# Issuing TensorE's instructions in program order in the loop over expert units

## The chip, the cores and the metric

The kernel runs on one core of one Trainium2 chip. The metric is the device time of one execution in microseconds (us). TensorE (PE in the profile, PEld for its weight loads) does the matrix products, VectorE (DVE) and ScalarE (ACT) the elementwise work, GpSimd (POOL) almost nothing here, and SyncE (SP) issues nearly all transfers from memory.

## The reference, cut to what matters

Two layers of a transformer-like block over 256 latent and 256 context tokens of width 1024, all in float32. Each layer has a mixer (a gated recurrence, a windowed attention and a gated chunk mixer) and a channel mixer. The change is in the channel mixer of the second layer, which picks two of eight experts for each of the 256 latent tokens:

```python
def _swiglu(h, w_gate, w_up, w_down):
    return (jax.nn.silu(h @ w_gate) * (h @ w_up)) @ w_down

def _moe(h, router, w_gate, w_up, w_down):
    logits = (t @ router).astype(jnp.float32)
    top_val, top_idx = lax.top_k(logits, TOP_K)
    top_w = jax.nn.softmax(top_val, axis=-1)
    gate = jnp.sum(one_hot(top_idx, 8) * top_w[..., None], axis=1)
    for e in range(N_EXPERTS):
        out = out + gate[:, e:e + 1] * _swiglu(t, w_gate[e], w_up[e], w_down[e])
```

An expert is 1024 -> 3584 -> 1024, so its three matrices are 44 MB, and each token needs only two experts.

## The kernel before

Only the tokens that chose an expert are gathered for it, up to 96 of them (`S`), in three blocks of 32. Whether an expert has more than 64 tokens is read at run time (`self.third[e]`), and every product of the loop stands twice in the program, in the two arms of an `If` (`arms`): one arm works on three blocks, the other leaves the third out.

The hidden width of an expert is cut into four **units** u = 0 to 3: three of 1024 hidden columns and one of 512 (`UNITS`). A unit goes through these steps:

- `gate_up` (G below): the gate and up products into three PSUM banks of kind `u`, in two halves, each an `If` of its own. A half reads 8 weight tiles of 512 KB (4 in the last unit). Then ACT and DVE make `mh`, silu(gate) times up.
- `turned` (T): eight transposes (L1620, L1625; four in the last unit) of `mh` into the two PSUM banks of kind `t`, copied out as `mT`.
- `moe_down` (D): the down product of `mT` with 8 weight tiles (4 in the last unit), in one `If`, into two banks of kind `mm` in which all units of the expert add up.

After an expert's last D, `moe_out` reads the two `mm` banks into `y` (ACT and DVE) and `moe_add` splits `y` into `yhl` and adds it to the tokens: eight products (L1682, m below) through the two `t` banks, each pair followed by a DVE addition into `xt` (L1684). `moe_gather` (g, o: L1827, L1564) picks the tokens of the next two experts, through the same two banks.

In the Python program, D of a unit is written one unit late: G of unit u, D of unit u-1, T of unit u. The pieces of `moe_add` and `moe_gather` are generators in the queue `behind`; `paced` runs one piece of them after each half of G and after each D.

That is the order in which the program is traced. The order in which an engine issues its instructions is chosen afterwards by the framework's scheduler; an `If` block is moved as a whole. So TensorE's order before need not be the program's.

The weights come through a ring of 4 KB-per-partition slots (`Ring`, L179): SP issues each load into a slot that earlier products have read, in the order of use that `moe_plan` writes down. 672 loads of 512 KB feed the loop.

Of the kernel before, what the change touches and what calls it, by code (L numbers as in the profile page):

```python
# [21 lines left out]
P = 128  # L22
# [5 lines left out]
NE = 8  # L28
# [168 lines left out]
class Gen:  # L197
# [1766 lines left out]
    def moe_layer(self):  # L1964
        nc, tc, mem = self.nc, self.tc, self.mem
        xg = {}
        self.third = [nc.values_load(self.cnt[0:1, 9 + e:10 + e], min_val=0, max_val=1)
                      for e in range(NE)]
        self.run(self.moe_gather(0, 2, xg, self.sel, self.rank, S, self.map0))
        behind = deque()  # L1970

        def paced(g):
            for _ in g:
                if behind and next(behind[0], self) is self:
                    behind.popleft()
        pend = y = None

        def lower():
            nonlocal y
            e, u, hT = pend  # L1980
            if u == 0:
                y = self.psum("mm"), self.psum("mm")
            paced(self.moe_down(e, hT, u, *y))
            if u == 3:
                behind.append(self.moe_add(self.moe_out(*y), xg[e][1], self.gate[:, :, e:e + 1], S, xg[e][2]))
        for e, u in self.UNITS:
            if u == 0 and e % 2 and e + 1 < NE:
                behind.append(self.moe_gather(e + 1, 2, xg, self.sel, self.rank))
            h = mem.get(4, [P, 2, 512], "mh")
            paced(self.gate_up(e, xg[e][0], u, h))  # L1990
            if u == 3:
                mem.put(xg[e][0])
            if pend:
                lower()
            pend = e, u, self.turned(h, u)
        lower()
        self.run(*behind)
        self.ring.close()
        self.store()
        with tc.If(nc.values_load(self.cnt[0:1, 8:9], min_val=0, max_val=256) > S):  # L2000
            self.moe_rest()
            self.store()
# [114 lines left out]
```

## Time and profile before

| what | before |
|---|---|
| median of 3 runs | 1904.02 us (1901.4 to 1908.13) |
| the profiled execution: its time, its span | 1906.77 us, 1905.0 us |
| busy share of the span: PE, PEld, DVE, ACT | 93%, 57%, 41%, 28% |
| mean granted clock of TensorE | 0.974 of full |
| the loop over expert units | about 937.5 to 1886 us of the span |

The span runs from the first to the last instruction. "Busy" of PE is the time in which some product runs. [...] A wait is idle time of an engine and what released it; "issue" is idle time for which the profile shows no releaser.

### The profile page before, as it was taken

Reading aid. Unit: us, or ns where it says so; the run is one execution under the profiler, and the core shown is the slowest. Engines: PE = TensorE matmul, PEld = TensorE weight load, DVE = VectorE, ACT = ScalarE, POOL = GpSimd, SP = SyncE. Lnnn points to the kernel's source line nnn. Section 1 sums busy time; section 2 is a strip of 40 time slices with the busy share of each in tenths; the row PEclk is TensorE's granted clock in tenths of the full one; section 3 lists DMA queues with packets and bytes.
Section 4 is the critical chain, followed back from the end, with each engine's and each line's share of the span. In section 5 each row is a group of like instructions: output and inputs, shape, how many; then the busy total and the mean of one; then the engine's idle time right before and its main releaser. Section 6 shows DMA issues by size and latency. Waiting matters only on the chain. (4 is left out here: it accounts for less than half of the span.)

```text
span 1905.0 us, 34709 instructions
## 1 busy us (share of the span) xinstructions
PE 1773.4 (93%) x14056; PEld 1088.7 (57%) x14057; DVE 778.7 (41%) x1924; ACT 538.5 (28%) x1203; POOL 33.9 (2%) x56
## 2 busy tenths in 40 slices
PE   6999999999999999999899978999789997899896
PEld 3998779988788899998534322233222332233232
DVE  3656887998563578778400112001120021100201
ACT  4654646622223367575200101001010010100000
POOL 1000000100000000000000000000000000000000
PEclk9999999999999999999999999999899998999898
DMA  9224242377562254312789999999998999999780
GB/s 337 78 85 166 82 155 89 116 256 263 163 249 97 90 173 137 133 47 105 289 314 407 407 407 408 345 359 408 407 385 321 355 408 407 370 345 373 302 332 25
DMA packets 137007, 485.65 MB, mean 255 GB/s; under 512 B 15888, under 2 KB 17040, under 8 KB 136784
## 3 DMA queue, kind: packets, MB, share of 16 engines
q1 hardware_dynamic: 136080, 480.08, 67.0%
q8 instruction: 168, 2.75, 0.6%
q0 software_dynamic: 704, 2.36, 0.4%
q14 instruction: 55, 0.45, 0.1%
HBM read 481.33 MB, written 1.05 MB: 253 GB/s over the span
## 5 line engine op out<-in xcount | busy, mean ns | idle before, releaser
L1575 PE MATMUL u<-wr,xg 128*32 128x512 f32 (+1 forms) x5376 | 535.5, 553 | 32.3 <-issue 28.2
L1575 PEld LDWEIGHTS u<-wr,xg 128*32 128x32 f32 x5376 | 179.9, 113 | 375.5 <-issue 335.6
L1608 DVE TENSOR_TENSOR mh<-mh,u 128x512 f32<-128x512 f32 (+1 forms) x32 | 19.9, 621 | 643.5 <-PE u L1575 643.5
L1575 PE MATMUL mm<-wr,mT 128*32 128x512 f32 x2352 | 263.2, 599 | 0.7 <-ACT mT L264 0.3
L264 ACT ACTIVATE mh<-u 128x512 f32<-128x512 f32 (+1 forms) x64 | 34.6, 540 | 751.7 <-PE u L1575 751.2
L125 ACT ACTIVATE hi<-raw 128x512 fp32r<-128x512 f32 (+2 forms) x296 | 160.2, 580 | 249.5 <-PE u L246 87.4
L126 DVE TENSOR_TENSOR lo<-raw,hi 128x512 fp32r<-128x512 f32 (+2 forms) x296 | 178.5, 634 | 100.5 <-ACT hi L125 99.1
L1575 PEld LDWEIGHTS mm<-wr,mT 128*32 128x32 f32 x2352 | 76.3, 111 | 169.4 <-issue 160.3
L244 PE MATMUL u<-hx,hi 128*128 128x512 f32 (+1 forms) x384 | 142.8, 372 | 0.0
L245 PE MATMUL u<-hx,lo 128*128 128x512 f32 (+1 forms) x384 | 142.6, 371 | 0.0
L246 PE MATMUL u<-hx,hi 128*128 128x512 f32 (+1 forms) x384 | 142.6, 371 | 0.0
L245 PE MATMUL mm<-fx,lo 128*128 128x256 f32 (+1 forms) x264 | 85.6, 325 | 5.7 <-DVE lo L126 5.5
L244 PE MATMUL mm<-hi,hx 128*128 128x256 f32 x288 | 85.4, 298 | 4.1 <-ACT hx L264 3.8
L244 PE MATMUL mm<-fx,hi 128*128 128x256 f32 (+1 forms) x264 | 85.0, 322 | 0.6 <-ACT hi L125 0.6
L246 PE MATMUL mm<-fx,hi 128*128 128x256 f32 (+1 forms) x264 | 84.6, 321 | 0.0
L245 PE MATMUL mm<-hi,hx 128*128 128x256 f32 x288 | 82.2, 287 | 0.4 <-DVE hx L521 0.3
L246 PE MATMUL mm<-lo,hx 128*128 128x256 f32 x288 | 81.6, 285 | 0.0
L245 PEld LDWEIGHTS u<-hx,lo 128*128 128x128 f32 x384 | 72.3, 188 | 12.6
L246 PEld LDWEIGHTS u<-hx,hi 128*128 128x128 f32 x384 | 72.3, 188 | 12.4
L244 PEld LDWEIGHTS u<-hx,hi 128*128 128x128 f32 x384 | 72.3, 188 | 12.4
L447 DVE SCALAR_TENSOR_TENSOR adat<-adat,silb 128x1024 f32<-128x1024 f32 x56 | 68.3, 1222 | 15.9 <-DMA adat<-in_w_adaT 15.1
L244 PE MATMUL u<-hi,hx 128*128 128x256 f32 x256 | 74.1, 290 | 0.1
(342 smaller groups left out, 2514.7 us busy)
## 6 DMA issues: line engine op xcount, KB each, us to landing
wr<-in_moe_g SPq DMA_DIRECT2D x224, 512.0 KB, 9.9
wr<-in_moe_u SPq DMA_DIRECT2D x224, 512.0 KB, 9.0
wr<-in_moe_d SPq DMA_DIRECT2D x224, 512.0 KB, 9.5
adat<-in_w_adaT SPq DMA_DIRECT2D x56, 512.0 KB, 4.9
raw<-in_ffn_gu SPq DMA_DIRECT2D x44, 512.0 KB, 3.5
adaw<-in_w_ada SPq DMA_DIRECT2D x40, 512.0 KB, 5.8
raw<-in_w_in SPq DMA_DIRECT2D x40, 512.0 KB, 3.8
raw<-in_ffn_d SPq DMA_DIRECT2D x24, 384.0 KB, 3.5
```

What stands on the lines that cost most here:

```text
L125: nc.scalar.activation(h[:, s], r[:, s], AF.Copy)
L126: nc.vector.tensor_tensor(l[:, s], r[:, s], h[:, s].bitcast(F32), op=ALU.subtract)
L244: i = mm(ps, lh, rh, start=start, stop=False, skip_group_check=True)
L245: mm(ps, ll, rh, start=False, stop=False, skip_group_check=True)
L246: self.final = mm(ps, lh, rl, start=False, stop=stop, skip_group_check=True)
L264: i = self.nc.scalar.activation(out, in_, func, **kw)
L447: nc.vector.scalar_tensor_tensor(w[i] if z == zs - 1 else junk, w[i], 1.0, sil[z], op0=ALU.mult, op1=ALU.mult, accum_out=self.mods[l][:, c ...
L1575: self.nc.tensor.matmul(bank[c:c + 32, :n], lhsT, rhs, start=start, stop=stop, tile_position=(0, c), skip_group_check=True)
L1608: nc.vector.tensor_tensor(h[:, 0, :n], h[:, 0, :n], U[:, :n], op=ALU.mult)
```

## The change

The loop over units is wrapped in a block that tells the framework to keep TensorE's instructions in the order in which they are traced. The statements in it are the same; the other engines are still ordered by the scheduler.

```diff
-        for e, u in self.UNITS:
-            if u == 0 and e % 2 and e + 1 < NE:
-                behind.append(self.moe_gather(e + 1, 2, xg, self.sel, self.rank))
-            h = mem.get(4, [P, 2, 512], "mh")
-            paced(self.gate_up(e, xg[e][0], u, h))
-            if u == 3:
-                mem.put(xg[e][0])
-            if pend:
-                lower()
-            pend = e, u, self.turned(h, u)
-        lower()
+        with tc.manual_schedule(engines={mybir.EngineType.PE}):
+            for e, u in self.UNITS:
+                if u == 0 and e % 2 and e + 1 < NE:
+                    behind.append(self.moe_gather(e + 1, 2, xg, self.sel, self.rank))
+                h = mem.get(4, [P, 2, 512], "mh")
+                paced(self.gate_up(e, xg[e][0], u, h))
+                if u == 3:
+                    mem.put(xg[e][0])
+                if pend:
+                    lower()
+                pend = e, u, self.turned(h, u)
+            lower()
```

TensorE's rows at the start of the third expert (e = 2), before: the end of the previous expert's last D, T of the new expert's unit 0, three products of `moe_add` for the expert just ended (`yhl` times `ohT`), and the first half of unit 1's G.

```order
L1575 MATMUL mm_104<-wr_12228,mT 32x512 x4
L1575 MATMUL mm_104<-wr_12230,mT 32x512 x4
L1580 UNCONDITIONAL_BRANCH
L1620 MATMUL t_106<-ident,mh 128x128 x4
L1625 MATMUL t_107<-ident,mh 128x64 x4
L1682 MATMUL t_106<-yhl,ohT 128x512
L1682 MATMUL t_107<-yhl,ohT 128x512
L1682 MATMUL t_106<-yhl,ohT 128x512
L1580 COMPARE_AND_BRANCH
L1575 MATMUL u_109<-wr_12232,xg 32x512 x2
L1575 MATMUL u_109<-wr_12234,xg 32x512 x2
```

The same place on TensorE now, where G of unit 1 follows T at once:

```order
L1575 MATMUL mm_104<-wr_12232,mT 32x512 x4
L1580 UNCONDITIONAL_BRANCH
L1620 MATMUL t_106<-ident,mh 128x128 x4
L1625 MATMUL t_107<-ident,mh 128x64 x4
L1580 COMPARE_AND_BRANCH
L1575 MATMUL u_109<-wr_12234,xg 32x512 x2
L1575 MATMUL u_109<-wr_12236,xg 32x512 x2
```

The products of `moe_add` have moved behind both halves of unit 1's G and behind its D, in two groups of four.

TensorE's rows one unit on, before: the end of unit 1's G, its T, and then D of unit 0.

```order
L1575 MATMUL u_111<-wr_12430,xg 32x512 x2
L1575 MATMUL u_111<-wr_12432,xg 32x512 x2
L1580 UNCONDITIONAL_BRANCH
L1620 MATMUL t_106<-ident,mh 128x128 x4
L1625 MATMUL t_107<-ident,mh 128x64 x4
L1580 COMPARE_AND_BRANCH
L1575 MATMUL mm_104<-wr_12434,mT 32x512 x4
L1575 MATMUL mm_104<-wr_12436,mT 32x512 x4
```

The same T on TensorE now: the end of unit 0's D, the second group of `moe_add`, T of unit 1, then G of unit 2.

```order
L1575 MATMUL mm_104<-wr_12535,mT 32x512 x4
L1580 UNCONDITIONAL_BRANCH
L1682 MATMUL t_106<-yhl,ohT 128x512 x2
L1682 MATMUL t_107<-yhl,ohT 128x512 x2
L1620 MATMUL t_106<-ident,mh 128x128 x4
L1625 MATMUL t_107<-ident,mh 128x64 x4
L1580 COMPARE_AND_BRANCH
L1575 MATMUL u_110<-wr_12537,xg 32x512 x2
L1575 MATMUL u_110<-wr_12539,xg 32x512 x2
```

T has moved from ahead of D to behind it. SP's loads of expert weights keep their order.

## Rows read from the trace of the kernel before

**Rows 1.** The page: span, and busy time, share, instructions by engine.

```profile
span 1905.0 us, 34709 instructions
PE 1773.4 (93%) x14056; PEld 1088.7 (57%) x14057; DVE 778.7 (41%) x1924; ACT 538.5 (28%) x1203; POOL 33.9 (2%) x56
```

**Rows 2.** Busy time by stretch: the eight experts in order, then the end.

```profile
core 0: us, PE busy (x) PEld busy (x) DVE busy (x) ACT busy (x) POOL busy (x), PEclk, DMA share, GB/s
937.50:1049.30 111.80, 110.44 (x1100) 39.76 (x1104) 6.75 (x13) 8.54 (x17) 0.00 (x0) 1.00 0.86 336
1049.30:1156.80 107.50, 93.70 (x821) 33.81 (x817) 15.31 (x24) 10.42 (x20) 0.00 (x0) 0.95 1.03 407
1156.80:1284.40 127.60, 118.50 (x1144) 41.57 (x1140) 15.59 (x26) 10.42 (x20) 0.00 (x0) 0.97 0.95 366
1284.40:1392.30 107.90, 93.06 (x820) 33.82 (x816) 15.31 (x24) 10.42 (x20) 0.00 (x0) 0.94 1.03 407
1392.30:1520.20 127.90, 118.67 (x1144) 41.59 (x1140) 15.59 (x26) 10.42 (x20) 0.00 (x0) 0.97 0.92 349
1520.20:1627.10 106.90, 92.63 (x820) 33.46 (x816) 15.31 (x24) 10.42 (x20) 0.00 (x0) 0.94 1.02 406
1627.10:1753.30 126.20, 116.25 (x1132) 39.14 (x1128) 14.56 (x22) 9.32 (x16) 0.00 (x0) 0.97 0.94 359
1753.30:1886.10 132.80, 123.95 (x1192) 41.15 (x1184) 14.57 (x22) 9.31 (x16) 0.00 (x0) 0.96 0.67 253
1886.10:1905.00 18.90, 4.52 (x8) 2.12 (x8) 8.01 (x10) 2.82 (x4) 0.00 (x0) 0.64 0.17 59
```

**Rows 3.** PE's waits from 937 to 1897 us: total, times, longest.

```profile
PE u L1575 <- issue: 28.2, 15, 3.7
PE t L1682 <- ACT yhl L264: 23.2, 4, 5.8
PE t L1620 <- DVE mh L1608: 18.4, 22, 1.0
PE t L1682 <- ACTq L2000: 5.6, 1, 5.6
PE u L1575 <- DMA wr<-in_moe_g: 4.1, 2, 3.1
PE t L1682 <- DVE xt L1684: 3.3, 8, 0.5
```

**Rows 4.** Timeline of ACT, DVE and PE around the first long wait of `moe_add`.

```profile
start us, us, engine line op out<-in xcount [idle before <-releaser]
1177.40 3.62 PE L1575 MATMUL mm<-wr,mT 128*32 128x512 f32 x32
...
1180.94 0.66 PE L1620 MATMUL t<-ident,mh 128*128 128x128 f32 x4
...
1182.49 1.39 DVE L1657 TENSOR_TENSOR y<-mm,gf 64x512 f32<-64x512 f32 x2
...
1185.45 1.22 DVE L1664 TENSOR_TENSOR y<-y,gf 32x1024 f32<-32x1024 f32 x1
1186.70 1.06 ACT L264 ACTIVATE yhl<-y 96x1024 fp32r<-96x1024 f32 x1 [2.60 <-DVE y L1664]
...
1187.81 2.05 PE L1682 MATMUL t<-yhl,ohT 96*128 96x512 f32 x3 [5.81 <-ACT yhl L264]
```

**Rows 5.** Windows: the four stretches of lower clock behind those waits.

```profile
1184.70:1191.50 6.80, 3.66 (x12) 1.20 (x16) 4.76 (x8) 1.06 (x1) 0.00 (x0) 0.50 1.03 410
1420.20:1427.00 6.80, 3.63 (x11) 1.18 (x15) 4.79 (x8) 1.06 (x1) 0.00 (x0) 0.50 1.00 400
1655.70:1662.60 6.90, 4.43 (x15) 1.38 (x19) 3.23 (x4) 1.06 (x1) 0.00 (x0) 0.51 0.93 369
1782.00:1792.30 10.30, 6.32 (x27) 1.89 (x31) 4.54 (x6) 1.29 (x2) 0.00 (x0) 0.50 0.60 240
sum 30.80, PE 18.05 PEld 5.65 DVE 17.32 ACT 4.46 POOL 0.00; mean PE 4.51 PEld 1.41 DVE 4.33 ACT 1.11 POOL 0.00
```

**Rows 6.** Timeline of ACT, DVE and PE around one T that waits.

```profile
1212.78 0.60 ACT L264 ACTIVATE mh<-u 128x512 f32<-128x512 f32 x1 [25.02 <-PE u L1575]
1212.95 0.61 PE L1575 MATMUL u<-wr,xg 128*32 128x512 f32 x4
...
1213.78 0.69 DVE L1608 TENSOR_TENSOR mh<-mh,u 128x512 f32<-128x512 f32 x1 [9.86 <-PE u L1575]
1214.50 0.69 DVE L1610 TENSOR_TENSOR mh<-mh,u 64x512 f32<-64x512 f32 x1
1214.52 0.66 PE L1620 MATMUL t<-ident,mh 128*128 128x128 f32 x4 [0.96 <-DVE mh L1608]
...
1215.64 10.51 PE L1575 MATMUL mm<-wr,mT 128*32 128x512 f32 x96
```

**Rows 7.** PE's timeline: the last G of expert 3, and two D's.

```profile
1354.90 8.77 PE L1575 MATMUL mm<-wr,mT 128*32 128x512 f32 x64
...
1366.33 2.35 PE L1575 MATMUL u<-wr,xg 128*32 128x256 f32 x37
1371.77 3.05 PE L1575 MATMUL u<-wr,xg 128*32 128x256 f32 x31 [3.08 <-issue]
1377.95 5.96 PE L1575 MATMUL u<-wr,xg 128*32 128x256 f32 x60 [3.13 <-issue]
...
1385.43 7.07 PE L1575 MATMUL mm<-wr,mT 128*32 128x512 f32 x64
```

**Rows 8.** DMA queues from 937.5 to 1886.1 us: packets, MB, share of 16 engines.

```profile
q1 hardware_dynamic: 92492, 336.77, 91.1%
q8 instruction: 120, 1.97, 0.8%
```

**Rows 9.** Busy time in the second half of expert 0 (columns as in rows 2).

```profile
995.00:1049.00 54.00, 52.94 (x572) 21.48 (x568) 3.37 (x7) 4.63 (x11) 0.00 (x0) 1.00 1.02 408
```

**Rows 10.** PE's waits in G by expert: 1, 3, then 5.

```profile
PE u L1575 <- issue: 9.7, 5, 3.6
...
PE u L1575 <- issue: 10.8, 5, 3.1
...
PE u L1575 <- issue: 7.1, 3, 3.7
PE u L1575 <- DMA wr<-in_moe_g: 3.1, 1, 3.1
```

## The prediction

> **What bounds the kernel now.** I began with the page: TensorE is busy for 93% of 1905.0 us, far ahead of DVE and ACT [rows 1]. That share is a mean over two layers, and the change touches only the loop over expert units, so the next view was busy time by stretch, one stretch per expert [rows 2]. Two kinds of expert alternate there. Experts 0, 2, 4, 6 and 7 take 112 to 133 us with 1100 to 1192 products (third block worked); experts 1, 3 and 5 take about 107 us with some 820 products. Expert 2 shows PE idle for 9 us of 127.6, expert 3 for 15 of 107.9; the granted clock falls to 0.94 to 0.97 in all but the first.
>
> Loads are the second candidate. Experts 1, 3 and 5 run with 406 to 407 GB/s, the highest rate in the table, and experts 2, 4, 6 with 349 to 366: there the queue has room. Over the loop 336.77 MB moved [rows 8]; at 407 GB/s that is 827 us of the loop's 948.6. So the loads alone would allow 121 us less; TensorE sets the pace, with the loads close behind in the short experts.
>
> Then PE's waits, longest total first [rows 3]. Three kinds matter:
> - 23.2 us in four waits of up to 5.8 us by the products of `moe_add` for `yhl`;
> - 18.4 us in 22 waits by T for `mh`;
> - 28.2 us in 15 waits of G for which no releaser is shown.
>
> The 5.6 us wait put down to ACT's sequencer is `moe_add` again, of the last expert, behind the loop's last D.
>
> **What the change does to the first kind.** Around one such wait [rows 4] the cause is plain. The last D of the expert ends at 1181, T follows, and then `moe_add` stands at the head of TensorE's queue while its input is only being made: `y` on DVE from 1182.5, a scaling until 1186.7, then ACT's copy; the product starts at 1187.8. All of G of the next unit stands behind it. In the new order two halves of G and nothing else stand in between: a half of 96 products is as long as the 96-product D of [rows 6], 10.5 us, so 21 us of work cover 7 us of latency. The four waits go: **-23.2 us**. The fifth stays, since nothing follows it in the loop.
>
> **The clock behind them.** [...]
>
> **The second kind.** T reads `mh`, which ACT and DVE make when G has ended. Before, T stands directly behind G and waits 0.96 us while silu and product finish [rows 6]; D, which needs nothing of this unit, stands behind T. Now D comes first and covers the wait ten times over. T's own copies `mT` are late by one D, but their reader is D of this unit, a whole G later. All 22 waits go except that one new one appears: in unit 0 of expert 0 there is no earlier D, so T follows G directly, and I charge it the 0.96 us of [rows 6]. **-18.4 + 1.0 = -17.4 us**.
>
> **What is moved next to it.** Four products of `moe_add`, in two pairs, now stand between D and T in some units. They share two PSUM banks with T, so T must wait for DVE's additions that read them. This already happens within `moe_add`: 3.3 us in eight waits [rows 3], 0.4 us each. The groups of four now start with both banks free, so these inner waits go, and four or five T's pay a little more than one such wait each. Taken as 0; bounds -3 and +4. The gather's products, which stood at the end of the even experts, are spread over the following odd one; they are work that stays.
>
> **The third kind, which the change does not aim at.** The 15 waits "issue" all sit inside a G. In the last G of expert 3, 128 products break after 37, wait 3.08 us, run 31, wait 3.13 us and run 60 [rows 7]; so they don't fall together with the limit between the halves, at 64, where the next weights are first read. During the loop a queue "instruction" fetched 120 packets of 1.97 MB in all [rows 8], 16 KB each, and the short experts pass over the arm with the third block. I read these waits as instruction pages that arrive late. The 4.1 us put down to `in_moe_g` [rows 3] have the same length and I count them alike: 32.3 us together. Since the number of instructions executed and skipped stays, I take 0. Bounds: they may go where the change puts other work between the halves of a fast G (-16, half of them), or grow, as faster work asks for pages sooner (+28, as much again).
>
> [...]
>
> **The loads, once TensorE is faster.** Expert 2 with expert 3 takes 127.6 + 107.9 = 235.5 us. An expert is 44 MB, two are 88 MB, 216 us at 407 GB/s. The gain falls mostly on the even experts: in 2 and 3 one long wait (5.8), one slow stretch (1.8) and six T waits (0.84 each on average, 5.0), 12.6 us, leave 223 us. That is still above 216, so the loads stay just hidden; the ring refills in the long expert and drains a little in the short one.
>
> **Sum.** -23.2 - 9.0 - 17.4 = -49.6 us. The profiled execution took 1906.8 us (span 1905.0 and 1.8 around it), 2.8 above the median of the runs. Taken off the profiled time that is 1857; taken off the median 1904.0 it is 1854.4. I say **1855 us**.
>
> **Rivals.**
> - *The forecast*, 1845 to 1868: the three terms, with the small ones either way. 60%. Within it lies the case that the loads bind in experts 1, 3 and 5 after all: their rate is at the top of the table already, their nine T waits (7.5 us) would then turn into waits for weights, and it ends at 1862.
> - *More comes back*, 1830 to 1845. Some half-clock stretches lie behind a late page and a T wait together: D of 64 products took 8.77 us there against 7.07 [rows 7], 1.7 us in each short expert. If T's part is what tips them, 5 us more; if half of the pages' waits go, 16 more: 1834. For it speaks that the two halves of the last unit's fast G, which run 3 us apart, get `moe_add` products between them; against it, that a page needs as long as before. 14%.
> - *Late pages take half back*. If the waits on pages grow by as much again, 28 us, it ends at 1883. For it: they occur almost only in experts 1, 3 and 5 [rows 10], where the queue moves 407 GB/s, and the other experts will come nearer to that rate. Against it: expert 0 ran at 408 GB/s from 995 to 1049 with PE busy for 52.94 of 54 us [rows 9]. 17%.
> - *It ends slower*: the same mechanism in all experts. Experts 1, 3 and 5 lose 9.7, 10.8 and 7.1 us to pages, and the last 3.1 more for `in_moe_g` [rows 10]: some 10 each. If the five long experts came to lose as much, that is 50 us and the gain is gone; past about 11.5 us in each, 56 in all, the kernel is measurably slower, and at 13 each it takes 1904 - 50 + 65 = 1919. Rows 9 speak against it. Slower 4%, no change 3%.
> - *It doesn't do what it says*: the order of the built program shows T behind D and `moe_add` behind G, so I give this 2%, counted as no change.
>
> **How the numbers follow.** A difference of 0.3%, 5.7 us, is about what a measurement here can tell from none. Faster is 60 + 14 + 17 = 91%; same 5%; slower 4%. The likeliest case alone is 1845 to 1868. For eight in ten the range has to take in most of the two neighbours: from 1834, where T's clock and half of the pages come back, to 1883, where late pages double.
>
> **What would show it.** In the profile after: no wait of `moe_add` for `yhl` over 1 us inside the loop (the last one stays at 5.6); T's waits for `mh` down from 22 to one; no stretch of 0.5 clock at the beginning of experts 2, 4, 6 and 7; the even experts near 115 us and the odd ones a little under 107, at 400 GB/s in both. It would be wrong if waits "issue" in G come to much more than 32 us, or if G begins to wait for `in_moe_g` and `in_moe_u` with the queue at 407 GB/s throughout. If T's waits return under another name, for DVE's `xt`, the term I took as 0 was mis-sized.

## The result, and the profile after

The changed kernel takes **1837.68 us** (median of 4 runs, 1835.17 to 1844.53) against 1904.74 us for the kernel before on the same chip: ratio 0.9654, 95% interval 0.9622 to 0.9685, so 67 us less. The forecast was 1855 with a range from 1834 to 1883. The time lies in the range, and outside the likeliest case (1845 to 1868): it is where the rival "more comes back" was put. The profiled execution took 1835.17 us.

The page after, to [rows 1]:

```profile
span 1833.4 us, 34728 instructions
PE 1753.2 (96%) x14056; PEld 1084.3 (59%) x14057; DVE 778.5 (42%) x1924; ACT 537.7 (29%) x1203; POOL 33.3 (2%) x56
```

The span is 71.6 us shorter, with the same number of products. TensorE is busy for 20.2 us less, and idle for 51.4 us less.

Busy time by expert after, to [rows 2] (same columns; of the eight experts 1, 2 and 7):

```profile
1045.90:1145.30 99.40, 90.85 (x834) 33.86 (x832) 15.22 (x24) 11.26 (x25) 0.00 (x0) 0.98 1.03 406
1145.30:1261.20 115.90, 114.71 (x1126) 39.60 (x1124) 15.48 (x26) 9.37 (x17) 0.00 (x0) 1.00 1.02 403
...
1694.30:1815.20 120.90, 120.31 (x1190) 40.83 (x1188) 14.67 (x23) 9.62 (x17) 0.00 (x0) 1.00 0.78 309
```

Experts 2, 4 and 6 take 116 us, as forecast (115), at full clock. The odd ones take 99 to 102 us where "a little under 107" was forecast: most of the gain that the forecast lacks lies there. Loads run at 402 to 406 GB/s in experts 1 to 6, where experts 2, 4 and 6 had 349 to 366.

PE's waits after, from 936 to 1826 us, to [rows 3]:

```profile
PE u L1575 <- issue: 14.6, 12, 3.4
PE t L1620 <- DVE mh L1608: 6.5, 4, 1.9
PE t L1682 <- ACTq L2001: 5.6, 1, 5.6
PE u L1575 <- DMA wr<-in_moe_g: 4.3, 2, 3.8
PE mm L1575 <- ACT mh L264: 1.5, 3, 0.6
PE t L1620 <- DVE xt L1684: 1.5, 4, 0.4
PE mm L1575 <- DMA wr<-in_moe_g: 1.1, 1, 1.1
PE u L1575 <- DMA wr<-in_moe_d: 0.6, 1, 0.6
PE mm L1575 <- DMA wr<-in_moe_d: 0.5, 1, 0.5
PE mm L1575 <- issue: 0.5, 1, 0.5
PE t L1682 <- DVE xt L1684: 0.4, 1, 0.4
```

The waits for `yhl` (23.2 us) are gone. T's waits for `mh` fell from 18.4 us in 22 to 6.5 us in four, not to the single one forecast; 1.5 us of waits for `xt` have come up. The waits in G, taken as unchanged at 32.3 us, fell to 14.6 + 4.3 = 18.9 us.

That is not all saved, for waits of the same kind came up elsewhere: 3.6 us inside D (the rows `mm`; 0.2 us before) and 0.6 us in G put down to `in_moe_d`. The trace has the packets of the instruction queue, 16 KB each (120 of them, 1.97 MB, in the 948.6 us of the loop before, one every 8 us on average). Before, every wait in G but one of 0.3 us at the loop's start ends 1.2 to 1.6 us after such a packet has landed: the wait that ends at 1371.77 [rows 7] has a packet from 1369.30 to 1370.33, the one that ends at 1377.95 a packet from 1375.51 to 1376.60. After, the rows above hold 21 waits in G and D, and all but the one at the loop's start end 1.3 to 1.8 us after a packet. So I count them all as waits for late instruction pages: 32.5 us before, 23.1 after, 9.4 less.

PE's timeline at the start of expert 2, where [rows 4] showed the wait of 5.81 us:

```profile
1170.57 0.66 PE L1620 MATMUL t<-ident,mh 128*128 128x128 f32 x4
...
1171.54 20.81 PE L1575 MATMUL u<-wr,xg 128*32 128x512 f32 x192
1192.28 1.19 PE L1682 MATMUL t<-yhl,ohT 96*128 96x512 f32 x4
```

T and both halves of G follow without a gap; 20.81 us of G cover what `moe_add` waited for (21 were forecast).

**Half clock.** The granted clock (PEclk in the windows, the share of full speed that TensorE was given) stands at 1.0 or at 0.5 in both traces, at no other level. Besides the four stretches of [rows 5] the kernel before had seven more in the loop at 0.5, all in experts 1, 3 and 5. The sum of their windows:

```profile
sum 37.40, PE 30.47 PEld 12.60 DVE 0.00 ACT 0.00 POOL 0.00; mean PE 4.35 PEld 1.80 DVE 0.00 ACT 0.00 POOL 0.00
```

After there are three such stretches, in the same experts:

```profile
sum 13.60, PE 12.51 PEld 5.25 DVE 3.19 ACT 1.72 POOL 0.00; mean PE 4.17 PEld 1.75 DVE 1.06 ACT 0.57 POOL 0.00
```

Work done at half clock was 18.05 + 30.47 = 48.5 us of busy time and is 12.5 now. I take half of that as lost (the first D of [rows 7], 3.4 us of it at 0.5, took 8.77 us against 7.07, 1.70 more), so 18.0 us came back, not the 9.0 of the forecast. That accounts for most of the 20.2 us of busy time.

**The waits of T that stayed.** Timeline in expert 1, to [rows 6]:

```profile
1068.37 1.57 PE L1827 MATMUL t<-oh,mhf 128*128 128x192 f32 x8
...
1069.97 0.55 ACT L264 ACTIVATE xg<-t 128x192 f32<-128x192 f32 x2 [6.23 <-PE t L1827]
1070.41 1.22 ACT L264 ACTIVATE mh<-u 128x512 f32<-128x512 f32 x2
1071.05 0.69 DVE L1608 TENSOR_TENSOR mh<-mh,u 128x512 f32<-128x512 f32 x1 [24.74 <-ACT mh L264]
...
1071.79 0.66 PE L1620 MATMUL t<-ident,mh 128*128 128x128 f32 x4 [1.85 <-DVE mh L1608]
```

G ended at about 1061.6, but ACT makes `mh` only at 1070.4: ahead of it in ACT's queue, which the scheduler orders, stand the gather's copies into `xg`, and the second pair of them needs products that TensorE runs after D. So D does not cover `mh` here. This happens in unit 0 of experts 1, 3 and 5, 1.9 us each.

The last G of expert 3, to [rows 7], where waits "issue" had cost 3.08 and 3.13 us, one in each half:

```profile
1339.29 1.93 PE L1575 MATMUL u<-wr,xg 128*32 128x256 f32 x30
1342.60 2.32 PE L1575 MATMUL u<-wr,xg 128*32 128x256 f32 x34 [1.38 <-issue]
1344.85 1.19 PE L1682 MATMUL t<-yhl,ohT 96*128 96x512 f32 x4
1349.47 3.66 PE L1575 MATMUL u<-wr,xg 128*32 128x256 f32 x64 [3.43 <-issue]
...
1355.35 7.07 PE L1575 MATMUL mm<-wr,mT 128*32 128x512 f32 x64 [1.08 <-DMA wr<-in_moe_g]
```

The waits in G are 1.38 and 3.43 us, 1.4 less, but 1.08 us of it comes up in the D behind; the 64 products of the second half run at full clock in 3.66 us (60 took 5.96). By expert, to [rows 10], the waits "issue" in G are now 2.2, 7.0 and 4.1 us in experts 1, 3 and 5 (9.7, 10.8 and 7.1 before). With the waits put down to weights and those in D it is 6.5, 8.1 and 4.7 us, against 9.9, 10.8 and 10.2. The instruction queue fetched as much as before, to [rows 8], while the loads' queue is busier (91.1% before):

```profile
q1 hardware_dynamic: 92451, 336.64, 96.9%
q8 instruction: 120, 1.97, 0.9%
```

### The profile page after: what moved, and what is told of

Its sections match the earlier page's. It is cut to its first block, busy times and chain, and to the rows that moved or that the text cites. A ratio compares the mean times of both kernels' runs of the same rounds, so it can differ in the third digit from the quotient of the medians.

```text
span 1833.4 us, 34728 instructions
## 1 busy us (share of the span) xinstructions
PE 1753.2 (96%) x14056; PEld 1084.3 (59%) x14057; DVE 778.5 (42%) x1924; ACT 537.7 (29%) x1203; POOL 33.3 (2%) x56
## 5 line engine op out<-in xcount | busy, mean ns | idle before, releaser
L1575 PE MATMUL u<-wr,xg 128*32 128x512 f32 (+1 forms) x5376 | 523.9, 545 | 19.7 <-issue 14.6
L1575 PEld LDWEIGHTS u<-wr,xg 128*32 128x32 f32 x5376 | 174.0, 111 | 342.2 <-issue 291.5
L264 ACT ACTIVATE mT<-t 128x512 f32<-128x512 f32 (+1 forms) x32 | 17.4, 544 | 256.3 <-PE t L1620 255.4
L1626 DVE COPY mT<-t 128x256 f32<-128x256 f32 (+1 forms) x32 | 12.5, 392 | 170.6 <-PE t L1625 170.6
```

What stands on the lines that cost most here:

```text
L264: i = self.nc.scalar.activation(out, in_, func, **kw)
L1575: self.nc.tensor.matmul(bank[c:c + 32, :n], lhsT, rhs, start=start, stop=stop, tile_position=(0, c), skip_group_check=True)
L1626: nc.vector.tensor_copy(hT[:, :m, :, 64:], pt[:, :m * 64].rearrange("p (j a s) -> p j a s", j=m, a=2))
```

## The experiments

**Theory.** Two places in the old order of TensorE cost the time: T directly behind its G, and `moe_add` directly behind T. Besides, instruction pages that arrive late cost time in both kernels. **Rivals.** Another part of the order is the cause; or the waits "issue" are no instruction pages; or the scheduler's order would have been as slow in any form of this program.

**1. T put back (e1_t_first).** The changed kernel, with T written ahead of D:

```diff
+                hT = self.turned(h, u)
                 if pend:
                     lower()
-                pend = e, u, self.turned(h, u)
+                pend = e, u, hT
```

> The changed kernel (1837.7 us), with one thing put back: in program order the transposes of a unit (T) stand ahead of the down product (D) of the unit before, so that nothing covers the making of mh where T follows G directly; moe_add and the gather stay in their new places. T follows G directly with nothing of moe_add or the gather between in four units of expert 0, one of each of experts 1, 3 and 5, and three of each of 2, 4, 6 and 7. Theory (T's waits are plain idle time): 0.6 to 1.0 us in each of these some 19 units, 17 us in all, against 6.5 us of such waits in the changed kernel, so 10 us slower, about 1848 us. Rival 1 (T's waits were also what brought the half clock in the short experts): more stretches of 0.5 clock return and it is 18 to 25 us slower, 1856 to 1863 us. Rival 2 (short waits of T cost nothing, as other work or the loads set the end): within 3 us of 1838.

Measured: 1877.82 us, ratio to the kernel before 0.9854 (0.9839 to 0.9870), 40 us above the changed kernel. The theory and both rivals fell: all of them are too low. PE's waits:

```profile
PE t L1620 <- DVE mh L1608: 38.3, 32, 1.9
PE u L1575 <- issue: 19.6, 16, 3.0
```

T waits in all 32 units, where 19 were expected, 1.2 us each; before the change it waited in 22. The other ten stood behind more work in the old order: in expert 0 the first T began at 968.5 us, 10.4 after the first silu of its `mh` had ended (957.49 + 0.60), with a half of the next unit's G in between. This kernel covers none of them, so it undoes more than the change did. Waits in G are 22.6 us in all (19.6 and 3.0 for `in_moe_g`), so T's place alone doesn't bring back the 32.3. T's waits are 31.8 us more; TensorE is also busy for 11.9 us more (1765.1), 3.6 of it for half clock (mean granted clock of the profiled executions 0.985 against 0.988), and the rest of that I have not traced.

**2. moe_add put back (e2_add_first).** Two steps of `moe_add` behind T of unit 0 in experts 2, 4, 6 and 7:

```diff
                 pend = e, u, self.turned(h, u)
+                if u == 0 and len(behind) == 1:
+                    for _ in range(2):
+                        next(behind[0], None)
```

> The changed kernel, with one thing put back: in experts 2, 4, 6 and 7 the first half of the products of moe_add stands directly behind T of unit 0, as before the change; T stays behind D. Theory: four waits of 5.8 us for yhl return (23 us), and behind each a stretch of half clock (9 us in all): 32 us slower than the changed kernel, about 1870 us. Rival 1: the clock doesn't fall behind them, since T's waits ahead of them were part of the cause: 23 us, 1861 us. Rival 2: the loads, which run at over 400 GB/s in the changed kernel from expert 1 on, are what sets its pace, and the waits are hidden: under 10 us slower.

Measured: 1873.47 us, ratio 0.9835 (0.9817 to 0.9853), 36 us above the changed kernel. PE's waits, and the sum of the windows of the four half-clock stretches behind them:

```profile
PE t L1682 <- ACT yhl L264: 23.2, 4, 5.8
PE u L1575 <- DMA wr<-in_moe_g: 11.6, 5, 3.8
PE u L1575 <- issue: 9.4, 11, 1.6
```

```profile
sum 37.40, PE 23.57 PEld 7.84 DVE 19.95 ACT 4.52 POOL 0.00; mean PE 5.89 PEld 1.96 DVE 4.99 ACT 1.13 POOL 0.00
```

The 23.2 us come back to the tenth, and half clock behind them for 23.57 us of work, 11.8 us lost (9.0 before the change). Together they are 35.0 of the 40.3 us by which the two profiled spans differ (1873.7 and 1833.4); 2.6 us more of half clock in experts 1, 3 and 5 and smaller terms are the rest (mean granted clock of the profiled executions 0.975 against 0.988). So it is shown that `moe_add` in this place makes these waits, and that the lower clock comes with them: at these four places nothing was changed but `moe_add`, which waits there, and the four stretches came back, at 0.50 in each window. What makes the clock fall there is not shown.

**3. Both put back (e9_both_first).** The two edits together.

> The changed kernel with both reversals at once, each written into the program order: T directly behind its G, and the first two groups of moe_add directly behind T of unit 0 in experts 2, 4, 6 and 7. Theory: these two places are all that the old order of TensorE cost, so the time returns to that of the kernel before, 1895 to 1915 us, with four waits of 5.8 us for yhl and more than 20 waits of T for mh. If the two costs were additive it would be 1837.7 + 40 + 36 = 1914. Rival: each of the two idle times covers late instruction pages that the other would leave open, or something else in the old order cost time too; then it ends below 1890, and a part of the 67 us has another cause that has not been named.

Measured: 1910.13 us, ratio 1.0028 (1.0009 to 1.0047), within 0.3% of the kernel before. PE's waits:

```profile
PE t L1620 <- DVE mh L1608: 35.8, 31, 1.9
PE t L1682 <- ACT yhl L264: 22.6, 4, 5.7
PE u L1575 <- issue: 20.3, 14, 3.0
```

The sum 1837.7 + 40 + 36 = 1914 holds within 4 us. But the composition isn't that of before: T waits 17 us more, and G 11 us less (20.3 + 1.1 against 32.3). So the theory's time held, but the agreement of the totals is partly chance, and something else in the old order made the waits in G longer.

**4. No Ifs (e3_fixed_arms).** The arm of each expert is fixed in the program:

```diff
     def arms(self, e):
-        with self.tc.If(self.third[e] > 0) as c:
-            yield 1
-        with c.Else():
-            yield 0
+        yield int(e in (0, 2, 4, 6, 7))
```

> The changed kernel without the If blocks of the products: which experts have a third block (0, 2, 4, 6, 7 for these inputs) is written into the program, so the arms that aren't executed and the branches around them are not there. It leaves out the choice at run time. Theory (the waits inside G without a releaser are late instruction pages, made by passing over the arm that isn't executed): these waits, 14.2 us for issue and 4.3 us put down to in_moe_g, fall to under 5 us together, the count of instruction packets in the loop falls from 120 to some 75, and the time falls by about 15 us to 1822 us; if the loads then bind in the short experts, waits for in_moe_g and in_moe_u of the same size as the gain stand there instead, at 406 GB/s. Rival (the weights are late): the waits stay where they are and the time stays within 4 us of 1838.

Measured: 1822.56 us, ratio 0.9573 (0.9558 to 0.9589), 15 us below the changed kernel. Its waits in G and D, and its instruction queue in the loop:

```profile
PE mm L1575 <- DMA wr<-in_moe_d: 4.3, 17, 1.1
PE u L1575 <- DMA wr<-in_moe_u: 3.3, 12, 0.5
...
q8 instruction: 64, 1.05, 0.5%
```

With 64 packets in place of 120 no wait "issue" in G or D is left, and no half clock in the loop. So, with the packets that land ahead of each of them, I take the waits without a releaser to have been for instruction pages. The gain is less than the 23.1 us of waits and the 6.3 us of half clock: 7.6 us of waits for weights have come up, and TensorE's busy time is 2.6 us higher (1755.8) instead of 6.3 lower, which I have not traced. The 64 packets that still came have no such wait behind them. The waits went with the passed-over arms; but where they stood, they stood inside a run of products (after 37 in [rows 7]), and no run here shows a branch and its page together.

**5. Split arms (e5_split_arms, e6_split_three).** The same idea with the choice left in: the first two blocks' products stand outside the `If`, the third block's alone in it.

```diff
+    def parts(self, e):
+        yield 0
+        with self.tc.If(self.third[e] > 0):
+            yield 1
...
-            for arm in self.arms(e):
+            for arm in self.parts(e):
...
                         if arm:
                             self.four(X, n, ((b2, ga), (b2, gb), (b2, ua), (b2, ub)), *z)
+                        else:
+                            self.four(G, n, ((b0, ga), (b1, ga), (b0, gb), (b1, gb)), *z)
+                            self.four(U, n, ((b0, ua), (b1, ua), (b0, ub), (b1, ub)), *z)
```

> The changed kernel (1837.7 us) with the products of the first two blocks taken out of the If, so that they stand once in the program and only the third block's products are conditional; the choice stays at run time. A half of G is then 128 instructions of its own and 64 in the If, where the two arms had 192 and 128. Five of the eight experts do four more products for a zero start of the third block's bank (0.9 us each, 4 us in all). Theory (late instruction pages, made by passing over the other arm): instruction packets in the loop fall from 120 to about 75, the waits inside G from 18.5 to under 6 us, the half clock behind them goes; 10 to 15 us faster than the changed kernel, about 1825 us. Rival: each If costs by itself, wherever its products stand, and nothing is gained: 1838 to 1842 us.

Measured: 1827.37 us, ratio 0.9584 (0.9568 to 0.9600), 10 us below the changed kernel. The instruction queue fetched 74 packets in the loop. No wait "issue" in G is left; waits for weights come to 3.2 + 2.9 us. The rival, that each If costs by itself, has a small part: 36 waits for TensorE's own sequencer (PEq) come to 6.6 us, 0.2 each. This is the fastest version here that keeps the choice at run time.

The same kernel in a single run:

> The same kernel as e5_split_arms once more, one look on its own, to see how far its profile repeats: span within 5 us of that of e5_split_arms.

It took 1825.65 us, within 2 us of the median.

**6. The scheduler's order without Ifs (e8_fixed_arms_before).** The edit of experiment 4 on the kernel before.

> The kernel before (1905 us) without the If blocks, as in e3_fixed_arms: which experts have a third block is written into the program, and the choice at run time is left out. With no blocks, the scheduler may order TensorE's instructions in another way than in the kernel before. Theory (the change's gain is 35 us from waits for data and the clock behind them, and the rest from pages that came late in the old order and not in the new): the waits inside G of 32 us go, with some 10 us of half clock, 1860 to 1866 us, and the gap to e3_fixed_arms (1822.6 us) is about 40 us. Rival (without blocks the scheduler's order is as good as the program's): within 8 us of e3_fixed_arms.

Measured: 1830.84 us, ratio 0.9604 (0.9585 to 0.9623). My theory fell: I expected the old waits to stay. The rival is nearly met, 8 us above experiment 4. PE's timeline behind the last D of expert 1 (L1617 and L1622 are T here, L1679 `moe_add`):

```profile
1160.48 1.09 PE L1575 MATMUL mm<-wr,mT 128*32 128x512 f32 x8
1161.50 0.55 PE L1617 MATMUL t<-ident,mh 128*128 128x128 f32 x3
...
1165.36 2.75 PE L1575 MATMUL u<-wr,xg 128*32 128x512 f32 x20
1168.14 0.73 PE L1679 MATMUL t<-yhl,ohT 96*128 96x512 f32 x2
```

Without blocks the scheduler puts T between products of D, and `moe_add` between products of G, in small pieces; T waits 0.6 us in all, and nothing waits for `yhl`. The pieces have a price: PE is busy for 1781.5 us, 25.7 more than in experiment 4. So the same scheduler without blocks has none of the long waits: the old order was bad for the blocks that it had to move whole.

**7. Split arms, the scheduler's order (e10_split_before).** The edit of experiment 5 on the kernel before.

> Split arms (the products of the first two blocks outside the If, the third block's alone in it), with TensorE's order left to the scheduler. Theory: the scheduler's old order was bad because an If block moves whole; with most products outside any block it weaves T into D of the unit before and moe_add between products of G, as it did with fixed arms, so there is no long wait for yhl, T waits a few us in all, and the time is that of split arms in program order, 1827 us, within 15 us (1820 to 1842). Rival: the small Ifs that are left still hold the order back, T or moe_add again stands where its data is late, and the time is 1850 to 1880.

Measured: 1854.39 us, ratio 0.9725 (0.9709 to 0.9741): the rival's time, 27 us above split arms in program order. PE's waits, and its timeline at the start of expert 2 (L1690 is `moe_add`):

```profile
PE t L1690 <- ACT yhl L264: 10.3, 4, 2.6
PE t L1632 <- DVE mh L1617: 6.0, 10, 0.6
```

```profile
1171.20 2.77 PE L1575 MATMUL u<-wr,xg 128*32 128x512 f32 x20
1176.55 0.73 PE L1690 MATMUL t<-yhl,ohT 96*128 96x512 f32 x2 [2.58 <-ACT yhl L264]
1177.21 1.91 PE L1575 MATMUL u<-wr,xg 128*32 128x512 f32 x12
```

Both stories are half right. The scheduler does weave here, but only 20 products of G stand ahead of `moe_add`, and it waits 2.58 us each time. The pieces cost time as well: 12 products of G take 1.91 us alone, 0.16 each, and 192 in a row 20.8, 0.11 each. PE's busy time on the page is 1781.7 us against 1764.4 in program order, 17.3 more; that this is all due to the pieces is my reading.

**8. ACT and DVE in program order too (e4_three_engines, e7_split_three_engines).**

```diff
-        with tc.manual_schedule(engines={mybir.EngineType.PE}):
+        with tc.manual_schedule(engines={mybir.EngineType.PE, mybir.EngineType.Activation, mybir.EngineType.DVE}):
```

> The changed kernel, with ACT and DVE kept in program order in the loop as well. In the changed kernel three T's (unit 0 of experts 1, 3 and 5) still wait 1.85 us for mh, because ACT's queue holds the gather's copies ahead of the two silu's, and those copies wait for products that stand behind D. Theory: with ACT in program order the silu's come between the copies, the three waits go and it is 5 us faster than the changed kernel, about 1832 us. Rival 1: another input becomes late, since the copies of T (mT) and the additions of moe_add now stand behind other work on ACT and DVE: the same time or slower. Rival 2: the loads set the pace of the short experts, and it is the same.

Measured: 1843.87 us, ratio 0.9679 (0.9666 to 0.9693), 6 us above the changed kernel. The theory fell; rival 1 has the time, but not the reason. T's waits for `mh` are down to the one of 1.0 us in expert 0, but waits in G are 24.9 + 5.6 us. PE's timeline in expert 1, at the place of the late T above:

```profile
1071.00 2.77 PE L1575 MATMUL u<-wr,xg 128*32 128x512 f32 x21
1076.75 7.04 PE L1575 MATMUL u<-wr,xg 128*32 128x512 f32 x43 [2.98 <-issue]
```

T, at 1069.76, no longer waits 1.85 us; G behind it now waits 2.98 us ("issue"), and again so in experts 3 and 5, each time with 3.4 us of half clock. In the changed kernel an instruction packet came during T's wait (1069.89 to 1070.96); here it comes only at 1074.18, during G's. I read G's wait as one for a page, and the wait for `mh` as having covered it. What starts the packet is not shown.

The same three engines with split arms, where no wait "issue" in G is left:

> The kernel of e5_split_arms with ACT and DVE in program order as well, as in e4_three_engines. There the three waits of T for mh (1.85 us each) went, and three waits of 2.98 us inside the next G came, each with a stretch of half clock. Theory (those were late pages that the waits of T had covered): with fewer pages nothing comes in their place, and this is 4 to 6 us faster than e5_split_arms. Rival 1 (ACT's and DVE's program order is worse by itself): slower than e5_split_arms by 5 us, as e4_three_engines was than the changed kernel. Rival 2 (loads bind by now): the same.

1828.45 us, ratio 0.9596 (0.9577 to 0.9614): nothing is gained over split arms (1827.37). But this is no test of the theory, since the three waits of 1.85 us are not in split arms at all. There T (its second group of transposes, L1632) waits in unit 0 of experts 1, 3 and 5 only for `xg`:

```profile
PE t L1632 <- ACT xg L264: 1.9, 3, 0.7
```

With the arms split, ACT makes `mh` ahead of the gather's copies (at 1062.93 in expert 1, where the changed kernel has 1070.41). With three engines in program order these waits are 0.6 us, so about 1 us was there to gain. Waits for weights, 3.7 + 2.7 us, are as in split arms.

**9. The short unit (e11_short_unit_whole, e12_short_unit_t_first).** The last unit's G has two halves of 64 short products. In the changed kernel four products of `moe_add` stand behind each half in experts 1, 3 and 5; before, the halves followed each other. The first kernel writes these eight products ahead of that G, and the second does so on top of experiment 1:

```diff
                 h = mem.get(4, [P, 2, 512], "mh")
+                if u == 3 and e % 2 and behind:
+                    for _ in range(2):
+                        next(behind[0], None)
                 paced(self.gate_up(e, xg[e][0], u, h))
```

> The changed kernel, with the eight products of moe_add that lie between and behind the two halves of the last, short unit's G in experts 1, 3 and 5 written ahead of that G, so that its two halves follow each other as in the kernel before. Theory: these products gave late instruction pages time, and that is where 13 us of waits in G and 9 us of half clock went that the forecast did not have. Then waits in G grow from 18.9 us to 27 or more, half clock grows by 5 us or more in these experts, and the time is 1848 to 1862 us. Rival: a page is late by the same amount wherever four products of moe_add stand, since loads at 400 GB/s and the passed-over arm set it; then the time stays at 1833 to 1843 us, and the cause of the 22 us is elsewhere in the old order (where the gather's products stand).

Measured: 1834.89 us, ratio 0.9625 (0.9612 to 0.9639). The theory fell and the rival held: the time is that of the changed kernel within 3 us. Waits in G fell to 10.4 + 3.5 + 0.5 us, but D behind them now waits 4.3 ("issue") + 2.8 (put down to `in_moe_g`) + 1.7 us (to `mh`). That is 23.2 together, as in the changed kernel (23.1): I read this as late pages that moved, with none added.

> The same, with T also directly behind its G in every unit, as in the earlier run of T alone (1877.8 us, waits in G 22.6 us). Theory: T's waits add up with those of the run above: 40 us on top of it, 1888 to 1902 us, with waits in G of 28 us or more. Rival: where T stands right behind G, its waits cover the late pages, and the time stays within 6 us of T alone, 1872 to 1884 us.

Measured: 1887.16 us, ratio 0.9903 (0.9886 to 0.9919), 9 us above T alone; the rival (to 1884) fell, and the theory (from 1888 us, 28 us of waits) is missed by a little. Waits in G are 23.6 + 4.1 = 27.7 us, 27.9 with D. PE's timeline of the short unit's G in expert 3:

```profile
1371.31 2.67 PE L1575 MATMUL u<-wr,xg 128*32 128x256 f32 x31 [3.12 <-issue]
1377.49 6.14 PE L1575 MATMUL u<-wr,xg 128*32 128x256 f32 x59 [3.51 <-issue]
```

These are [rows 7] over again, and a half-clock stretch of 10.2 us lies on them as before (from 1372.3). In experts 1, 3 and 5 half clock is 37.4 us in seven stretches, as before the change, though not all at the same places; it is 13.6 in the changed kernel, 17.0 with T alone and 3.4 with the short unit alone. The mean granted clock (median over the runs of each kernel) has the same order: 0.980, 0.985, 0.984 and 0.989. Neither edit does it alone; with T behind G and the short unit whole, that half clock and the longest of the old page waits are back in experts 1, 3 and 5.

## Why the prediction was right, and what it had wrong

**What bounds the kernel, and the loads.** Right. TensorE sets the pace, and the loads stayed hidden at 402 to 406 GB/s, but with less room than forecast: experts 2 and 3 together took 217.7 us, where 223 was forecast and 216 was worked out for the loads. With the pages gone, experiments 4 and 5 wait 6 to 8 us for weights.

**moe_add, -23.2 us.** Right: 23.2 to 0, shown by experiment 2. The fifth wait, of 5.6 us behind the loop's last D, stayed as forecast.

**Half clock, -9.0 us.** That the four stretches go with the waits was right, the size was not: -18.0. The 9.0 us are an estimate, half of the 18.05 us of busy time in [rows 5]; no run shows this term by itself, and what the runs showed in its place is 11.8 us behind the same four waits (experiment 2) and 18.0 us in the whole loop. The step that was mis-sized counted only the four stretches behind `moe_add`. Seven more lay in experts 1, 3 and 5; the forecast had named them in the rival, as stretches that T's part might tip. Experiment 9 (its second kernel) shows that they do hang on T's place, but together with the short unit's.

**T, -18.4 + 1.0 us.** Mis-sized: 18.4 to 6.5, and 1.5 us of waits for `xt` came up, so -10.4. The new wait in expert 0 is there (0.9 us). What failed is "D covers the wait ten times over": it followed TensorE's queue, but not ACT's, where `mh` stands behind the gather's copies in three units. Experiment 8 shows it, since program order on ACT and DVE removes these three waits. It also shows that nothing was to gain there, for a wait of 2.98 us, which I read as a late page, came in place of each. The `xt` waits, taken as 0 with bounds -3 and +4, come to -2.9 within `moe_add` (3.3 to 0.4) and +1.5 at T.

**Late pages, taken as 0.** The reading held (experiments 4 and 5, with 64 and 74 packets, have no wait "issue" in G), the size did not: -9.4 with the waits that moved into D (-13.4 in G alone), inside the bound of -16. It gave as its reason that the number of instructions stays, and that number did stay, 120 packets; but the waits that I count for pages were 32.5 us in the old order and 23.1 in the new. The rival's reason, `moe_add` between the halves of the short G, isn't enough by itself (experiment 9, first kernel: 23.2 us). It takes T's place as well (second kernel: 27.9 us against 23.1 after and 32.5 before). Why these two act together I did not test; the 4.6 us that are left aren't traced either.

**The sum.** -23.2 - 18.0 - 10.4 - 2.9 - 9.4 = -63.9, against -71.6 in the span. Another 3.0 us are short waits of TensorE for copies out of the shared banks (`mT`, `xg`), which the forecast did not have: 3.2 before, 0.2 after. The last 4.7 are not traced. The forecast of 1855 missed by 17 us, and its range held only because its lower end took in most of a rival: "more comes back" described what came, with both its parts, 9 us of clock and 9 of pages; it got 14%. A slip without consequence: 56 us over five experts are 11.2 each, not 11.5. Of the list of what would show it, the waits for `yhl`, the clock at the start of the even experts, and their length held; the count of T's waits did not.

## What to carry to other kernels

Where blocks that can't be divided stand in a loop, read the scheduler's order of the busiest engine against the program's: a small operation whose input is late may stand in front of a long block that needs nothing of it. Putting one such operation back, `moe_add`, cost 36 us here; T, the other, waited 18.4 us in the old order. Taking the work that is common to both arms out of the `If` was worth another 10 us: fewer instructions are passed over, and the loop fetched 74 packets in place of 120. When a wait is costed at "covered", follow the queue of the engine that makes the input too; and a short wait may be worth nothing, as in experiment 8, where 2.98 us of "issue" came in place of each 1.85. When waits fall in one place, look whether they came up in another under another name, as the page waits did in D.

## What the runs showed that I had not expected

- Waits hid each other across causes: taking away three waits of 1.85 us for data was followed by three of 2.98 us that I read as waits for instructions, and the kernel got 6 us slower (experiment 8).
- The scheduler's order is good with no blocks (1830.84 us against 1822.56 in program order), though TensorE is busy for 25.7 us more there, and for 17.3 more with split arms, where long runs of products are cut into pieces of four to twenty (experiments 6 and 7).
- The two reversals add up to the old time (1910 us) with a different make-up of waits (experiment 3), so an equal total alone had not settled the cause.
